# FFN down-projection of a one-core transformer layer computed as seven Strassen block products, with two plain column pairs at the head of each FFN

## The chip, the cores and the metric

The kernel runs on one core of one Trainium2 chip. The metric is the device time of one execution in microseconds (us); smaller is better. The engines are named as the profile names them: PE (TensorE, matrix products), PEld (its weight loads), DVE (VectorE), ACT (ScalarE), POOL (GpSimd), SP (SyncE, whose queue issues all bulk transfers of this kernel). Each runs its own instructions in a fixed order and waits for the others by semaphores.

## The reference, cut to what matters

One layer on 1024 tokens of width 1024, all in float32: a half-weighted SwiGLU FFN, a token mixer (two attention branches, unchanged here), and a second half-weighted FFN, each behind an RMS norm, and a final norm.

```python
D_MODEL, SEQ, D_FF = 1024, 1024, 2816

def swiglu(h, w1, w3, w2):
    return (jax.nn.silu(h @ w1) * (h @ w3)) @ w2
...
    x = x + 0.5 * swiglu(rmsnorm(x, ffn1_norm), ffn1_w1, ffn1_w3, ffn1_w2)
    x = x + token_mix(rmsnorm(x, mix_norm), ...)
    x = x + 0.5 * swiglu(rmsnorm(x, ffn2_norm), ffn2_w1, ffn2_w3, ffn2_w2)
    return rmsnorm(x, final_norm)
```

## The kernel before, in words

Activations lie transposed: features on the 128 partitions, tokens along the free axis, in two token halves `tb` of 512. The width 1024 is KD = 8 tiles of 128; the hidden width 2816 is NF = 22 tiles `f`, taken as 11 pairs. Every product is made with a number split in two: `split` writes a rounded `hi` (ACT, line 86) and the rest `lo` (DVE, line 82), and hi·hi + hi·lo + lo·hi makes three matmuls of 128x128 by 128x512 (`mm3`, lines 49 to 51).

An FFN has an up stage (`ffn_up`) and a down stage (`ffn_down`).

- Up stage. The first f pair is plain: 2 halves x 2 f x 2 matrices x 8 k x 3 = 192 matmuls. Its first half uses the input before it is scaled by the RMS factor R (R multiplies the result); then `scale_h` scales the second half and the first, and `right_sums` makes the input sums that Strassen's scheme (Winograd's form) needs (`T`, tiles `tf`). Pairs 1 to 10 follow as seven block products of 24 matmuls each, 168 per pair, into PSUM banks X, Y and Z; the weight sums of a pair are made by POOL (lines 327 to 330), on DVE in the first such pair. `finish_a` multiplies the gate (line 349, POOL). The results `a` go to DRAM (`s_a`).
- Down stage. For each half, for each of 22 f: load `a` (256 KB) and the rows of w2 (512 KB), split both, and add into 8 PSUM accumulators: 2 x 22 x 8 x 3 = 1056 matmuls. The last three f of a half are held back (`L_LAST`) and run one accumulator at a time, so that each can be added to x (line 412) and passed on (norm statistics, or the final output) while the next runs.

The order on every engine is set at build time by a scheduler, from the program's order, priorities and its own estimate of times; buffers come free as the last reader finishes (pools). Waits inside SP's queue hold back every transfer behind them.

Of the kernel before, what the change touches and what calls it, by code (L numbers as in the profile page):

```python
# [125 lines left out]
def norm_split(K, tb, k, gi):  # L126
    nc = K.nc
    x = K.x[tb][k]
    g = K.gain[:, gi, k:k + 1]
# [2 lines left out]
    nc.scalar.activation(out=hi, in_=x, func=AF.Copy, scale=g)
# [9 lines left out]
def norm_stat(K, tb, k, eng=None, hold=False):  # L142
    nc = K.nc
    x = K.x[tb][k]
    if k == 0:
        K.acc[tb] = K.np.tile([P, TB], F32, tag="nacc", name="nacc")
        nc.scalar.activation(out=K.acc[tb], in_=x, func=AF.Square)
    else:
        sq = K.np.tile([P, TB], F32, tag=f"nsq{tb * K.sq2}", name="nsq")
# [1 line left out]
        (eng or nc.gpsimd).tensor_tensor(out=K.acc[tb], in0=K.acc[tb], in1=sq, op=ALU.add)
# [4 lines left out]
def norm_final(K, tb):
    nc = K.nc
    with K.tc.high_priority(offset=HOT):
        tot = K.pt.tile([P, TB], F32, tag="acc", name="tot")
        nc.tensor.matmul(tot, lhsT=K.ones, rhs=K.acc[tb], start=True, stop=True)  # L160
# [4 lines left out]


def tail_stat(K, c, k):
    nc = K.nc
# [3 lines left out]
    if k == 0:
        K.tacc = sq
    elif k < KD - 1:
        nc.vector.tensor_tensor(out=K.tacc, in0=K.tacc, in1=sq, op=ALU.add)
# [74 lines left out]
def ffn_up(K, w13, tp, ctx0, gi, first):  # L250
# [12 lines left out]
    def store(f, tb, t):  # L263
        nc.sync.dma_start(out=K.s_a[tb][f], in_=t)

    with ExitStack() as c1:
        sb = open_pool(K, c1, "up_s", 3, side="right")
        ws = first if first else [load_fresh(K, n, w13[n // 2, n % 2]) for n in range(4)]
        K.nw = 4
        for tb in range(NTB):  # L270
            for f in range(2):
                u = [bank("XY"[f], m) for m in range(2)]
                for m in range(2):
                    for k in range(KD):
# [8 lines left out]
                nc.vector.tensor_tensor(out=t, in0=u[1], in1=t, op=ALU.mult)  # L283
# [4 lines left out]
    ctx0.close()
    with ctx:
        rw = open_pool(K, ctx, "up_raw", 1)  # L290
        po = open_pool(K, ctx, "up_post", 1)
        raw = lambda n: rw.tile([P, KD, P], F32, tag=n, name=n)
        B11, B21, B22 = K.h[0][0:h], K.h[0][h:], K.h[1][h:]

        def prod(o, w, m, x, start):
            for k in range(h):
                for i, (a, b) in enumerate(((0, 0), (0, 1), (1, 0))):
                    nc.tensor.matmul(o, lhsT=w[a][:, m * h + k], rhs=x[k][b], start=start and k == 0 and i == 0,  # L298
                                     stop=k == h - 1 and i == 2, skip_group_check=True)
# [55 lines left out]

def ffn_down(K, w2, xsrc, after, tail):
    nc = K.nc
    with ExitStack() as ctx:
# [8 lines left out]
        K.wpools = K.wpools + [open_pool(K, ctx, "whl3", B_W, side="right")]  # L367
        queue = []

        def fetch():  # L370
# [1 line left out]
            if n < NTB * NF:
                t = ar.tile([P, TB], F32, tag="ar", name="ar")
                nc.sync.dma_start(out=t, in_=K.s_a[n // NF][n % NF])
                a = [ah.tile([P, TB], F32R, tag=g, name=g) for g in ("ah", "al")]
                split(nc, a[0], a[1], t)
                queue.append((load_fresh(K, n, w2[n % NF]), a))
        fetch()
        fetch()
        for tb in range(NTB):  # L380
            acc = None
            held = []
            for f in range(NF):
                fetch()
                w, a = queue[tb * NF + f]
                if f >= 2 and f % 2 == 0 and f // 2 <= KD:
                    k = f // 2 - 1
                    nc.sync.dma_start(out=K.x[tb][k], in_=xsrc(tb, k))
                if acc is None:
                    acc = [pa.tile([P, TB], F32, tag="acc", name="acc") for _ in range(KD)]  # L390
                if f < NF - L_LAST:
                    late = tb == 1 and f < 2
                    for d in range(KD - late):
                        mm3(nc, acc[d], w, d, a, f == 0, False, True)
                    if late:
                        held.append((w, a))
                        if f == 1:
                            norm_final(K, 0)
                            if tail is not None:
                                tail(0, slice(0, TB))  # L400
                            for i, (w, a) in enumerate(held):
                                mm3(nc, acc[KD - 1], w, KD - 1, a, i == 0, False, True)
                            held = []
                else:
                    held.append((w, a))
            cols = [slice(0, TB)] if tail is None or tb == 0 else [slice(0, HB), slice(HB, TB)]
            for c in cols:
                for d in range(KD):
                    for i, (w, a) in enumerate(held):
                        mm3(nc, acc[d][:, c], w, d, [t[:, c] for t in a], False, i == L_LAST - 1, True)  # L410
                    x = K.x[tb][d][:, c]
                    nc.vector.scalar_tensor_tensor(out=x, in0=acc[d][:, c], scalar=0.5, in1=x, op0=ALU.mult, op1=ALU.add)
                    if tail is None or tb == 0:
                        after(tb, d)
                    else:
# [1016 lines left out]
```

## Time and profile before

| what | value |
|---|---|
| time, median of 3 runs (lowest to highest) | 3072.87 us (3072.54 to 3073.18) |
| the profiled execution, its own time | 3074.79 us |
| its span (first to last instruction in the profile) | 3072.7 us |
| mean granted clock of TensorE | 0.982 |
| PE / DVE / ACT / POOL busy, share of the span | 95% / 60% / 41% / 27% |
| FFN 1: first matmul, first down matmul, last down matmul's end | 6.52, 475.58, 721.44 us |
| FFN 2: first up matmul, first down matmul, last down matmul's end | 2357.76, 2811.34, 3058.58 us |

Between 721 and 2358 us lie the mixer and the projections, which the change does not touch. A matmul row's duration in this profile is its time in the pipeline; the next starts long before it ends, so what a matmul costs is read from starts, not from durations.

### The profile page before, as it was taken

To read this page: it belongs to the slowest core of one execution; us is meant where nothing else is said; L and a number is where in the kernel's file an instruction comes from. 1 tells how busy PE (TensorE), PEld (TensorE's weight loads), DVE (VectorE), ACT (ScalarE), POOL (GpSimd) and SP (SyncE) were. 2 spreads that over 40 slices of the span, in tenths; PEclk is the share of its full clock that TensorE was granted. 3 is DMA by queue.
4 is the path that set the end of the run, shared out by engine and by line. 5 is a ranking of instruction groups with operands and counts; after the bars stand their busy time and mean duration, and the time that the engine had idled before them with its cause. 6 is when DMAs were issued, how large, how long until landed. Compare 5 with 4: busy or idle time off the path is not lost.

```text
span 3072.7 us, 39792 instructions
## 1 busy us (share of the span) xinstructions
PE 2925.8 (95%) x14490; PEld 2442.3 (79%) x14490; DVE 1838.1 (60%) x3057; ACT 1267.6 (41%) x2231; POOL 842.3 (27%) x687
## 2 busy tenths in 40 slices
PE   6999999999999999889899999999999899999998
PEld 5788887887888778777788888888777688887887
DVE  7655554445678467667677777766434855555354
ACT  6222223332323245345566666666434322223342
POOL 5333330000035222322233333222332433331000
PEclk9999999999999999999999999999999999999999
DMA  2222226444546645444432234222832122225442
GB/s 103 93 83 83 82 69 235 159 144 140 158 158 224 214 142 181 162 168 155 140 111 83 83 123 149 83 76 89 303 124 91 56 83 83 82 83 199 154 167 66
DMA packets 168643, 397.95 MB, mean 130 GB/s; under 512 B 16000, under 2 KB 34688, under 8 KB 168448
## 3 DMA queue, kind: packets, MB, share of 16 engines
q1 hardware_dynamic: 168448, 395.42, 38.0%
q8 instruction: 114, 1.87, 0.3%
q14 instruction: 81, 0.66, 0.1%
HBM read 274.77 MB, written 120.59 MB: 129 GB/s over the span
## 4 chain that ended last, share of the span: by engine, by line
PE 78%; DVE 8%; DMA 6%; ACT 3%; issue 3%; POOL 2%; SPq 1%; DVEq 0%; ACTq 0%; POOLq 0%
PE Y L298 11%; PE X L298 7%; PE Z L298 7%; PE gm L49 6%; PE gm L51 6%; PE gm L50 6%; PE S L682 6%; PE acc L49 5%; PE acc L51 5%; PE acc L50 5%; PE tr L732 3%; PE o L886 2%; PE o L885 2%; DMA sg<-smx 1%; DMA wst<-in_win_dram 1%
## 5 line engine op out<-in xcount | busy, mean ns | idle before, releaser
L82 DVE TENSOR_TENSOR wlo<-wst,whi 128x1024 fp32r<-128x1024 f32 x183 | 238.1, 1303 | 233.6 <-ACT whi L86 223.3
L49 PE MATMUL gm<-hi,whi 128*128 128x512 f32 x880 | 352.5, 401 | 4.6 <-ACT whi L86 2.1
L51 PE MATMUL gm<-hi,wlo 128*128 128x512 f32 x880 | 348.9, 397 | 0.0
L50 PE MATMUL gm<-lo,whi 128*128 128x512 f32 x880 | 348.6, 396 | 0.0
L682 PE MATMUL S<-kt,qt 128*128 128x320 f32 (+5 forms) x1152 | 274.5, 352 | 44.2 <-ACT Pt L691 16.5
L298 PE MATMUL Y<-tf,whi 128*128 128x512 f32 x960 | 300.2, 394 | 1.0 <-ACT whi L86 1.0
L86 ACT ACTIVATE whi<-wst 128x1024 fp32r<-128x1024 f32 x147 | 155.1, 1058 | 333.0 <-PE acc L50 187.3
L86 ACT ACTIVATE th<-tr 128x512 fp32r<-128x512 f32 (+2 forms) x384 | 204.0, 543 | 200.9 <-PE tr L732 196.5
L82 DVE TENSOR_TENSOR tl<-tr,th 128x512 fp32r<-128x512 f32 (+2 forms) x384 | 236.6, 620 | 82.6 <-ACT th L86 78.9
L49 PE MATMUL acc<-ah,whi 128*128 128x512 f32 (+1 forms) x728 | 280.4, 385 | 4.5 <-DVE u L342 4.5
L51 PE MATMUL acc<-ah,wlo 128*128 128x512 f32 (+1 forms) x728 | 280.3, 385 | 0.0
L50 PE MATMUL acc<-al,whi 128*128 128x512 f32 (+1 forms) x728 | 279.7, 384 | 0.0
L689 DVE CUSTOM_DVE_ANT_0 S<-S,slab 128x896 f32<-128x896 f32 (+7 forms) x320 | 224.9, 709 | 69.3 <-PE S L682 64.0
L682 PEld LDWEIGHTS S<-kt,qt 128*128 128x128 f32 x1152 | 183.5, 190 | 67.8 <-ACT Pt L691 17.7
L839 POOL TENSOR_SCALAR Ps<-Ps,l 128x384 f32<-128x384 f32 (+7 forms) x128 | 100.7, 787 | 422.3 <-DVE l L837 209.9
L298 PEld LDWEIGHTS Y<-tf,whi 128*128 128x128 f32 x960 | 180.7, 188 | 43.0 <-ACT whi L86 1.4
L86 ACT ACTIVATE whi<-a 128x1024 fp32r<-128x1024 f32 x100 | 104.0, 1058 | 233.4 <-PE Y L298 157.7
L49 PEld LDWEIGHTS gm<-hi,whi 128*128 128x128 f32 x880 | 168.6, 192 | 37.5 <-ACT whi L86 2.3
L51 PEld LDWEIGHTS gm<-hi,wlo 128*128 128x128 f32 x880 | 168.2, 191 | 36.0 <-DVE wlo L82 0.3
L50 PEld LDWEIGHTS gm<-lo,whi 128*128 128x128 f32 x880 | 168.3, 191 | 31.5 <-issue 0.5
L82 DVE TENSOR_TENSOR wlo<-a,whi 128x1024 fp32r<-128x1024 f32 x100 | 173.9, 1753 | 26.3 <-ACT whi L86 26.3
L298 PE MATMUL Y<-tf,wlo 128*128 128x512 f32 x480 | 188.6, 394 | 0.0
(302 smaller groups left out, 6683.4 us busy)
## 6 DMA issues: line engine op xcount, KB each, us to landing
wst<-in_win_dram SPq DMA_DIRECT2D x55, 512.0 KB
wst<-in_f1w_dram SPq DMA_DIRECT2D x48, 512.0 KB
wst<-in_f2w_dram SPq DMA_DIRECT2D x48, 512.0 KB
ar<-sa SPq DMA_DIRECT2D x88, 256.0 KB
a<-in_f1w_dram SPq DMA_DIRECT2D x40, 512.0 KB
a<-in_f2w_dram SPq DMA_DIRECT2D x40, 512.0 KB
qt<-sq SPq DMA_DIRECT2D x128, 128.0 KB
qt<-sqn SPq DMA_DIRECT2D x64, 256.0 KB
```

What stands on the lines that cost most here:

```text
L49: first = nc.tensor.matmul(out, lhsT=w[0][:, wk], rhs=x[0], start=start, stop=False, skip_group_check=skip)
L50: nc.tensor.matmul(out, lhsT=w[0][:, wk], rhs=x[1], start=False, stop=False, skip_group_check=skip)
L51: nc.tensor.matmul(out, lhsT=w[1][:, wk], rhs=x[0], start=False, stop=stop, skip_group_check=skip)
L82: return nc.vector.tensor_tensor(out=lo, in0=src, in1=hi.bitcast(F32), op=ALU.subtract)
L86: nc.scalar.activation(out=hi, in_=src, func=AF.Copy)
L298: nc.tensor.matmul(o, lhsT=w[a][:, m * h + k], rhs=x[k][b], start=start and k == 0 and i == 0, stop=k == h - 1 and i == 2, skip_group_chec ...
L682: K.last = nc.tensor.matmul(S[:, o:o + n], lhsT=q, rhs=k[:, k0 + c:k0 + c + n], start=i == 0, stop=i == 1)
L689: nc.vector.tensor_tensor_reduce(out=sv, in0=sv, in1=mv, scale=-0.125, scalar=BIG, op0=ALU.add, op1=ALU.min, accum_out=nm)
L732: nc.tensor.transpose(tr[:, b * P:(b + 1) * P], src, K.ident)
L839: nc.gpsimd.tensor_scalar(out=p[:, 0:n], in0=p[:, 0:n], scalar1=l[:, c:c + 1], scalar2=1.0, op0=ALU.mult, op1=ALU.mult)
L885: nc.tensor.matmul(dst, lhsT=v, rhs=hi[:, b * P:(b + n) * P], start=False, stop=False, skip_group_check=True)
L886: nc.tensor.matmul(dst, lhsT=v, rhs=lo[:, b * P:(b + n) * P], start=False, stop=last, skip_group_check=True)
```

## The change

The down-projection becomes Strassen's seven products too, over the blocks (f of a pair) x (half of the output width) on the left and (f of the pair) x (token half) on the right. One product runs over all 11 pairs before the next begins ("streamed"), into four accumulators: 7 x 11 x 4 x 3 = 924 matmuls per FFN. The sums it needs are made during the up stage: `left_sums` loads both w2 tiles of a pair, makes S1 to S4 on DVE and writes them back to DRAM (`s_w`); `act_sums` makes T1 to T4 of the activations on POOL and writes them to `s_a`; for the plain pairs `plain_sums` reads the activations back first. The down stage loads per step two blocks of 256 KB into one buffer, so that one ACT and one DVE instruction of 1024 elements split both. Outputs are added to x from one or two of the products each (`outs`), 36 additions of 128x512 (or their halves) per FFN for 16. The norm statistics no longer need the order k = 0 to 7.

`NPLAIN = 2`: two f pairs are plain, 384 matmuls, in the order (half, pair) = (0,0), (0,1), (1,1), (1,0); Strassen pairs are 2 to 10.

```diff
+NPLAIN = 2
+def load_plain(K, pools, n, src):
+    st = K.wst.tile([P, KD, P], F32, tag="wst", name="wst")
+    K.nc.sync.dma_start(out=st, in_=src)
+    pool = pools[n % 2] if n < 4 else pools[2]
...
+    split(K.nc, hi, lo, st)
-        for tb in range(NTB):
+        ws = [first if first else [load_plain(K, plain, n, w13[n // 2, n % 2]) for n in range(4)]]
+        ws.append([load_plain(K, plain, n, w13[n // 2, n % 2]) for n in range(4, 8)])
+        for tb, p in ((0, 0), (0, 1), (1, 1), (1, 0)):
             for f in range(2):
-                u = [bank("XY"[f], m) for m in range(2)]
+                u = [bank("XYZ"[nu % 3], m) for m in range(2)]
...
-            if tb == 0:
-                scale_h(K, 0, gi, scale_h(K, 1, gi))
+            if (tb, p) == (0, 0):
+                gates = scale_h(K, 1, gi)
+            if (tb, p) == (0, 1):
+                scale_h(K, 0, gi, gates)
+        jobs = [lambda j=j: left_sums(K, ex, w2, j) for j in range(NF // 2)]
+        jobs[4:4] = [lambda p=p: plain_sums(K, ex, p) for p in range(NPLAIN)]
-        for fp in range(1, NF // 2):
+        for fp in range(NPLAIN, NF // 2):
...
+            for job in jobs[done[0]:done[1]]:
+                job()
...
-                finish_a(K, u[n, 0], u[n, 1], f, 1, store)
+                finish_a(K, u[n, 0], u[n, 1], f, 1, store if n == "u3" else lambda *_: None)
+            act_sums(K, u["c11", 0], u["u2", 0], u["c21", 0], u["u3", 0], u["c21", 1], u["u2", 1], u["u3", 1], fp)
+def act_sums(K, b11, b12, b21, b22, t1, t2, t4, j):
+    for out, a, b, n in ((t1, b12, b11, "T1"), (b12, b22, b12, "T3"), (t2, b22, t1, "T2"), (t4, b21, t2, "T4")):
+        nc.gpsimd.tensor_tensor(out=out, in0=a, in1=b, op=ALU.subtract)
+        nc.sync.dma_start(out=K.s_a[n][j], in_=out)
+def left_sums(K, ex, w2, j):
+    for i in range(2):
+        w.append(ex.tile([P, KD, P], F32, tag=f"w{i}", name="w2s"))
+        order_after(K, nc.sync.dma_start(out=w[i], in_=w2[2 * j + i]), K.mark)
+    a11, a21, a12, a22 = w[0][:, 0:h], w[0][:, h:], w[1][:, 0:h], w[1][:, h:]
+    for out, a, b, op in ((a22, a21, a22, ALU.add), (a21, a11, a21, ALU.subtract), (a11, a22, a11, ALU.subtract),
+                          (a12, a12, a11, ALU.subtract)):
+        nc.vector.tensor_tensor(out=out, in0=a, in1=b, op=op)
+    for i in range(2):
+        nc.sync.dma_start(out=K.s_w[j][i], in_=w[i])
+PRODUCTS = (("A11", "B11", ((0, 0),)), ("S2", "T2", ((1, 0),)), ("S3", "T3", ((0, 1), (1, 1))),
+            ("A12", "B21", ((0, 0),)), ("A22", "T4", ((0, 1),)), ("S1", "T1", ((1, 0), (1, 1))), ("S4", "B22", ((1, 0),)))
 def ffn_down(K, w2, xsrc, after, tail):
...
+            st = raws[n % 2].tile([P, KD, P], F32, tag="wst", name="st")
+            nc.sync.dma_start(out=st[:, 0:h], in_=src[0][:, src[1] * h:(src[1] + 1) * h])
+            nc.sync.dma_start(out=st[:, h:], in_=K.s_a[r][j].rearrange("p (k c) -> p k c", c=P))
+            hi, lo = [pools[n % 4].tile([P, KD, P], F32R, tag=t, name=t) for t in ("whi", "wlo")]
+            split(nc, hi, lo, st)
...
+        for pi, (l, r, outs) in enumerate(PRODUCTS):
+            if pi not in (1, 2):
+                acc = [pa.tile([P, TB], F32, tag="acc", name="acc") for _ in range(h)]
+            for j in range(nj):
+                fetch()
...
+                if j < nj - L_LAST:
+                    for d in range(h):
+                        mm3(nc, acc[d], w, d, a, j == 0 and pi not in (1, 2), False, True)
...
+                    for tb, i in outs:
+                        x = K.x[tb][i * h + d][:, c]
+                        nc.vector.scalar_tensor_tensor(out=x, in0=acc[d][:, c], scalar=0.5, in1=x, op0=ALU.mult, op1=ALU.add)
```

What the scheduler makes of it, at three places. In the rows, names end in a number that tells buffers apart.

PE where the first half of the plain part of FFN 1 ends, before: the next matmuls read `hi_531`, the scaled tile of the second token half.

```order
L49 MATMUL Y_475<-hi_349,whi_336 128x512
L50 MATMUL Y_475<-lo_350,whi_336 128x512
L51 MATMUL Y_475<-hi_349,wlo_337 128x512
L49 MATMUL X_618<-hi_531,whi_271 128x512
L49 MATMUL X_619<-hi_531,whi_271 128x512
L49 MATMUL Y_672<-hi_531,whi_314 128x512
```

The same place now: after pair 0 (bank Z) comes pair 1 of the same half, with the unscaled tiles `hi_342`, `lo_343` again and new weights.

```order
L49 MATMUL Z_565<-hi_415,whi_402 128x512
L50 MATMUL Z_565<-lo_416,whi_402 128x512
L51 MATMUL Z_565<-hi_415,wlo_403 128x512
L49 MATMUL X_660<-hi_342,whi_486 128x512
L50 MATMUL X_660<-lo_343,whi_486 128x512
L51 MATMUL X_660<-hi_342,wlo_487 128x512
```

What moved: 96 matmuls that need no R stand between the unscaled and the scaled half.

POOL in a Strassen pair of the up stage, before: three gate products of a pair (`u3`, `c21`, `u2`; line 349), then the weight sums of the pair after the next (lines 327 to 330).

```order
L349 TENSOR_TENSOR c21_1081<-c21_1081,c21_1082 128x512
L349 TENSOR_TENSOR u3_1079<-u3_1079,u3_1080 128x512
L349 TENSOR_TENSOR u2_1077<-u2_1077,u2_1078 128x512
L327 TENSOR_TENSOR s1_1567<-a21_1565,a22_1566 128x1024
L328 TENSOR_TENSOR a21_1565<-a11_1563,a21_1565 128x1024
```

POOL in a Strassen pair now (408 is the gate product, 378 the activation sums, 352 on the weight sums):

```order
L408 TENSOR_TENSOR u2_1677<-u2_1677,u2_1678 128x512
L378 TENSOR_TENSOR c21_1682<-u2_1677,c11_1683 128x512
L378 TENSOR_TENSOR u2_1677<-u3_1679,u2_1677 128x512
L378 TENSOR_TENSOR u2_1678<-u3_1679,c21_1682 128x512
L378 TENSOR_TENSOR u3_1680<-c21_1681,u2_1678 128x512
L352 TENSOR_TENSOR s1_2217<-a21_2215,a22_2216 128x1024
L353 TENSOR_TENSOR a21_2215<-a11_2213,a21_2215 128x1024
```

What moved: T1, T3, T2, T4 stand between the last gate product and the weight sums, written over the pair's own work tiles (`c21`, `u2`, `u3`), which the next pair writes again.

SP in a Strassen pair, before (307 loads the weights w13, 264 stores results):

```order
L307 DMA a12_2311<-in_f1w13_dram 128x1024
L264 DMA sa1_10_203<-u2_1824 128x512
L307 DMA a21_2312<-in_f1w13_dram 128x1024
L307 DMA a22_2313<-in_f1w13_dram 128x1024
L264 DMA sa0_12_183<-c11_2079 128x512
```

SP there now (332 loads w13, 279 stores results, 379 the activation sums):

```order
L332 DMA a12_2214<-in_f1w13_dram 128x1024
L332 DMA a21_2215<-in_f1w13_dram 128x1024
L379 DMA saT1_4_219<-c21_1682 128x512
L379 DMA saT3_4_241<-u2_1677 128x512
L379 DMA saT2_4_230<-u2_1678 128x512
L379 DMA saT4_4_252<-u3_1680 128x512
L332 DMA a22_2216<-in_f1w13_dram 128x1024
L279 DMA saB11_5_176<-c11_1959 128x512
```

What moved: the load of a22 for a later pair stands behind four stores that wait for POOL; before, it followed that of a21 at once.

More of the change, by code (lines that the diff above doesn't have):

```diff
@@ L144, in norm_stat @@
     x = K.x[tb][k]
-    if k == 0:
+    if tb not in K.seen:
+        K.seen[tb] = 0
         K.acc[tb] = K.np.tile([P, TB], F32, tag="nacc", name="nacc")
@@ L151, in norm_stat @@
         (eng or nc.gpsimd).tensor_tensor(out=K.acc[tb], in0=K.acc[tb], in1=sq, op=ALU.add)
-    if k == KD - 1 and not hold:
+    K.seen[tb] += 1
+    if K.seen[tb] == KD and not hold:
         norm_final(K, tb)
@@ L169, in tail_stat @@
     x = K.x[1][k][:, c]
-    sq = K.np.tile([P, HB], F32, tag="tsq0" if k == 0 else f"tsq{k % 3 + 1}", name="tsq")
+    acc = K.acc[1][:, c]
+    sq = K.np.tile([P, HB], F32, tag=f"tsq{k % 2}", name="tsq")
     nc.scalar.activation(out=sq, in_=x, func=AF.Square)
[L172 to L175, printed above, removed]
+    if k < KD // 2 - 1:
+        nc.vector.tensor_tensor(out=acc, in0=acc, in1=sq, op=ALU.add)
     else:
         tot = K.pt.tile([P, TB], F32, tag="acc", name="tot")[:, 0:HB]
-        nc.tensor.matmul(tot, lhsT=K.ones, rhs=K.tacc, start=True, stop=False)
+        nc.tensor.matmul(tot, lhsT=K.ones, rhs=acc, start=True, stop=False)
         nc.tensor.matmul(tot, lhsT=K.ones, rhs=sq, start=False, stop=True)
-        m = K.np.tile([P, HB], F32, tag="tsq1", name="nm")
+        m = K.np.tile([P, HB], F32, tag="tsq0", name="nm")
         nc.vector.tensor_scalar(out=m, in0=tot, scalar1=1.0 / D, scalar2=EPS, op0=ALU.mult, op1=ALU.add)
-        newton_rsqrt(nc, K.R[1][:, c], K.tacc, m, nc.vector)
+        newton_rsqrt(nc, K.R[1][:, c], acc, m, nc.vector)
 def split_fresh(K, n, src):
@@ L247, in right_sums, with ffn_up @@
     return T
-def ffn_up(K, w13, tp, ctx0, gi, first):
+def load_plain(K, pools, n, src):
+    st = K.wst.tile([P, KD, P], F32, tag="wst", name="wst")
+    K.nc.sync.dma_start(out=st, in_=src)
+    pool = pools[n % 2] if n < 4 else pools[2]
+    hi = pool.tile([P, KD, P], F32R, tag="whi", name="whi")
+    lo = pool.tile([P, KD, P], F32R, tag="wlo", name="wlo")
+    split(K.nc, hi, lo, st)
+    return hi, lo
+NPLAIN = 2
+def ffn_up(K, w13, w2, ctxt, ctx0, gi, first):
     nc = K.nc
@@ L297, in prod @@
                 for i, (a, b) in enumerate(((0, 0), (0, 1), (1, 0))):
-                    nc.tensor.matmul(o, lhsT=w[a][:, m * h + k], rhs=x[k][b], start=start and k == 0 and i == 0,
-                                     stop=k == h - 1 and i == 2, skip_group_check=True)
-        for fp in range(1, NF // 2):
+                    K.mark = nc.tensor.matmul(o, lhsT=w[a][:, m * h + k], rhs=x[k][b], start=start and k == 0 and i == 0,
+                                              stop=k == h - 1 and i == 2, skip_group_check=True)
+        for fp in range(NPLAIN, NF // 2):
             f0, f1 = 2 * fp, 2 * fp + 1
@@ L330, in ffn_up @@
             se.tensor_tensor(out=s4, in0=a12, in1=a11, op=ALU.subtract)
+            done = (fp - NPLAIN) * len(jobs) // (NF // 2 - NPLAIN), (fp + 1 - NPLAIN) * len(jobs) // (NF // 2 - NPLAIN)
+            for job in jobs[done[0]:done[1]]:
+                job()
             for src, x, n in ((a11, T[1], "u2"), (a21, T[2], "u3"), (a22, T[3], "c21")):
@@ L361, in ffn_down @@
         K.x = [[xp.tile([P, TB], F32, name=f"xd{tb}_{k}") for k in range(KD)] for tb in range(NTB)]
-        ar = open_pool(K, ctx, "ar", 4, side="right")
-        ah = open_pool(K, ctx, "ah", L_LAST + 3, side="right")
+        pools = K.wpools + [open_pool(K, ctx, f"whl{i}", B_W, side="right") for i in (3, 4)]
+        raws = [K.wst, open_pool(K, ctx, "wst2", 2, side="right")]
         pa = open_pool(K, ctx, "acc", 8, True)
@@ L371, in fetch @@
             n = len(queue)
[L372 to L381, printed above, removed]
+            if n == len(PRODUCTS) * nj:
+                return
@@ L382, in ffn_down @@
+            hi, lo = [pools[n % 4].tile([P, KD, P], F32R, tag=t, name=t) for t in ("whi", "wlo")]
+            split(nc, hi, lo, st)
+            queue.append(((hi, lo), [t[:, h:].rearrange("p k c -> p (k c)") for t in (hi, lo)]))
+        for _ in range(3):
+            fetch()
+        acc = None
+        for pi, (l, r, outs) in enumerate(PRODUCTS):
             held = []
-            for f in range(NF):
+            if pi not in (1, 2):
+                acc = [pa.tile([P, TB], F32, tag="acc", name="acc") for _ in range(h)]
+            for j in range(nj):
@@ L384, in ffn_down @@
                 fetch()
[L385 to L403, printed above, removed]
+                w, a = queue[pi * nj + j]
@@ L404, in ffn_down @@
+                if pi < 3 and j < h:
+                    for tb, i in outs:
+                        nc.sync.dma_start(out=K.x[tb][i * h + j], in_=xsrc(tb, i * h + j))
+                if j < nj - L_LAST:
+                    for d in range(h):
+                        mm3(nc, acc[d], w, d, a, j == 0 and pi not in (1, 2), False, True)
                 else:
                     held.append((w, a))
-            cols = [slice(0, TB)] if tail is None or tb == 0 else [slice(0, HB), slice(HB, TB)]
@@ L407, in ffn_down @@
-            for c in cols:
-                for d in range(KD):
+                if pi == 5 and j == 4:
+                    norm_final(K, 0)
+                    if tail is not None:
+                        tail(0, slice(0, TB))
+            last = pi == len(PRODUCTS) - 1
+            for c in [slice(0, HB), slice(HB, TB)] if last and tail is not None else [slice(0, TB)]:
+                for d in range(h):
                     for i, (w, a) in enumerate(held):
                         mm3(nc, acc[d][:, c], w, d, [t[:, c] for t in a], False, i == L_LAST - 1, True)
[L411 to L415, printed above, removed]
+                    for tb, i in outs:
+                        x = K.x[tb][i * h + d][:, c]
+                        nc.vector.scalar_tensor_tensor(out=x, in0=acc[d][:, c], scalar=0.5, in1=x, op0=ALU.mult, op1=ALU.add)
+                    if pi in (3, 4, 5):
+                        after(int(pi == 5), d + h * (pi != 3))
+                    elif last and tail is None:
+                        after(1, d)
+                    elif last:
@@ L416, in ffn_down @@
                         tail_stat(K, c, d)
-                    if d == KD - 1 and tail is not None and tb:
-                        tail(tb, c)
+                if last and tail is not None:
+                    tail(1, c)
 def ffn(K, w13, w2, ctx0, gi, first, xsrc, after, tail=None):
@@ L425, in ffn @@
         with ExitStack() as c1:
-            ffn_up(K, w13, open_pool(K, c1, "tf", 1, side="right"), ctx0, gi, first)
+            ffn_up(K, w13, w2, c1, ctx0, gi, first)
         ffn_down(K, w2, xsrc, after, tail)
@@ L1258, in body @@
     K.tc, K.nc, K.A = tc, nc, A
-    K.low, K.vv, K.gate, K.fill = 0, {}, None, None
+    K.low, K.vv, K.gate, K.fill, K.seen = 0, {}, None, None, {}
     K.h, K.acc, K.R = [None] * 2, [None] * 2, [None] * 2
```

46 lines of the change are left out of this document (33 added, 13 removed).

## Prediction

> **What bounds the kernel now.** I read the page's first part and the chain, then PE's starts in the timeline, then PE's waits stage by stage. PE is busy 95% of the span and carries 78% of the chain; the other engines have room.
>
> ```profile
> PE 2925.8 (95%) x14490; PEld 2442.3 (79%) x14490; DVE 1838.1 (60%) x3057; ACT 1267.6 (41%) x2231; POOL 842.3 (27%) x687
> PE 78%; DVE 8%; DMA 6%; ACT 3%; issue 3%; POOL 2%; SPq 1%; DVEq 0%; ACTq 0%; POOLq 0%
> L298 PE MATMUL Y<-tf,whi 128*128 128x512 f32 x960 | 300.2, 394 | 1.0 <-ACT whi L86 1.0
> ```
>
> The 394 ns of that group is a matmul's time in the pipeline, not its price. The price comes from the chain in order of time: the same run of 24 X matmuls stands once per Strassen pair, so two of its starts, seven pairs apart, give the period.
>
> ```profile
> 168.23 5.52 PE X L298 x24
> ...
> 439.57 5.52 PE X L298 x24
> ...
> 2503.99 5.52 PE X L298 x24
> ```
>
> (439.57 - 168.23) / 7 = 38.76 us for 168 matmuls: **230.7 ns each**.
>
> Stage limits, from PE's timeline (start, duration, idle before):
>
> ```profile
> 6.52 1.22 PE L49 MATMUL X<-hi,whi 128*128 128x512 f32 x2 [6.52 <-ACT hi L132]
> ...
> 475.58 0.39 PE L49 MATMUL acc<-ah,whi 128*128 128x512 f32 x1
> ...
> 478.82 0.50 PE L49 MATMUL acc<-ah,whi 128*128 128x512 f32 x1 [2.27 <-DVE u L342]
> ...
> 726.37 1.22 PE L160 MATMUL tot<-nacc,ones 128*128 128x512 f32 x1 [4.93 <-DVE nacc L151]
> ...
> 2357.76 0.47 PE L49 MATMUL X<-hi,whi 128*128 128x512 f32 x1
> ```
>
> Down stage of FFN 1: from 475.58 to 726.37 - 4.93 = 721.44 is 245.9 us; less the wait of 2.27, 1056 matmuls take 243.6: 230.7 ns again. So both large stages run at PE's pace. What PE loses lies at the head of each FFN (waits by releaser: us, times, longest), the first four of FFN 1, the rest of FFN 2:
>
> ```profile
> PE X L298 <- DVE wlo L82: 7.4, 1, 7.4
> PE X L49 <- ACT hi L86: 7.3, 1, 7.3
> PE X L49 <- ACT hi L132: 6.5, 1, 6.5
> PE Y L49 <- DVE s L283: 6.0, 1, 6.0
> ...
> PE Z L298 <- ACT whi L86: 4.5, 1, 4.5
> PE X L50 <- DVE lo L82: 4.3, 2, 4.1
> PE X L298 <- DVE s L283: 4.0, 1, 4.0
> ```
>
> After such a wait PE also runs slow for some us; in the stage table (PE, PEld, DVE, ACT, POOL busy, PEclk, DMA share, GB/s) the granted clock falls to half:
>
> ```profile
> 40.00:50.00 10.00, 3.64 (x7) 2.12 (x8) 10.00 (x10) 9.67 (x19) 8.38 (x6) 0.50 0.07 26
> 80.00:90.00 10.00, 9.85 (x31) 7.83 (x32) 9.25 (x14) 2.98 (x6) 1.24 (x1) 0.71 0.42 140
> ```
>
> The loss as a whole: to the X run of the third Strassen pair stand 192 + 2 x 168 + 12 = 540 matmuls, 124.6 us, and four `tot` products (about 0.45 each; two in FFN 2). FFN 1 takes 168.23 - 6.52 = 161.7, **35.3 more**; FFN 2 takes 2503.99 - 2357.76 = 146.2, **20.7 more**.
>
> **The change, part by part.**
>
> *Down stage, matmuls.* 1056 - 924 = 132 fewer per FFN, 264 x 0.2307 = **-60.9 us**, if PE stays the limit. The Trainium skill (TensorE: Matmul & The Clock Gate, Back-to-back issue gap) gives two other prices for 512 columns, about 216 ns isolated and about 131 ns in a sustained stream; by these the 264 would be worth 57 or 35 us. The trace shows neither (230.7 in both stages), and decides. A step is now 12 matmuls, 2.77 us, and in it DVE splits 1024 elements, ACT too:
>
> ```profile
> L82 DVE TENSOR_TENSOR wlo<-wst,whi 128x1024 fp32r<-128x1024 f32 x42 | 52.0, 1239 | 108.3 <-ACT whi L86 108.3
> L412 DVE SCALAR_TENSOR_TENSOR xd<-acc,xd 128x512 f32<-128x512 f32 x16 | 11.0, 688 | 8.6 <-PE acc L51 8.6
> L86 ACT ACTIVATE whi<-wst 128x1024 fp32r<-128x1024 f32 x43 | 45.4, 1059 | 117.0 <-PE acc L50 102.2 <-DMA wst<-in_f1w_dram 14.7
> ```
>
> DVE: 11 x 1.239 + at most 8 x 0.688 = 19.1 us per product of 30.5. ACT: 11.6. POOL idle. Transfers: 2 x 256 KB per 2.77 us is 189 GB/s; the trace has shown 347 at this very place:
>
> ```profile
> 476.00:500.00 24.00, 21.73 (x94) 17.46 (x95) 12.80 (x16) 11.16 (x13) 1.29 (x1) 1.00 0.98 347
> ```
>
> The 16 loads of x (256 KB each, in SP's queue among steps 11 to 19) add 4 MB, 12 us at that rate; eight split buffers and four raw ones let the loads run ahead. I cost both at 0; with a cover gone the bound is 12 us per FFN.
>
> *Product boundaries.* Products 2 and 3 go on in the accumulators that DVE has just read, so PE could wait for the fourth addition, up to one split and one addition, 1.9 us, at two places per FFN. Other work of the next step stands before it on PE. Between 0 and 7.7; I take **+2**. The wait of 2.27 at the second accumulator goes: the first accumulator that waits for DVE is now the fourth, 2.1 us later in PE's order. Between 0 and -4.5; I take **-4.5**.
>
> *Second plain pair.* 192 - 168 = 24 matmuls more per FFN: 48 x 0.2307 = **+11.1**. It puts 96 matmuls, 22.1 us, ahead of the first that needs scaled input. Will that cover the scaling? R of the second half, DVE's scaling and splitting, and the end of PE's first 96 in FFN 1, and the first scaling in FFN 2:
>
> ```profile
> 35.55 0.69 DVE L122 TENSOR_TENSOR R<-R,nacc 128x512 f32<-128x512 f32 x1
> ...
> 38.26 8.81 DVE L209 SCALAR_TENSOR_TENSOR x<-x,gain,R 128x512 f32<-128x512 f32 x8
> ...
> 47.59 10.94 DVE L82 TENSOR_TENSOR lo<-x,hi 128x512 fp32r<-128x512 f32 x10
> ...
> 32.45 0.39 PE L51 MATMUL Y<-hi,wlo 128*128 128x512 f32 x1
> ...
> 2372.64 2.45 DVE L209 SCALAR_TENSOR_TENSOR xx<-xx,gain,R 128x512 f32<-128x512 f32 x2
> ```
>
> Four more weight splits on DVE (4 x 1.24, some in its gaps) put R at about 39. Begun at 41, the eight scalings end at 50 and the eight `lo` at 60, one per 1.1 us. PE ends its first 96 at 32.8 as before and 192 at 55; the `lo` are needed from 55 to 60, one per 0.7 us. It is covered by a hair. In FFN 2 the same splits, 5.0, and a plain result that now stands ahead of R put the scaling at about 2381, its end 20 us later at 2401; PE needs it from 2357.8 + 192 matmuls and two `tot` = 2403. So nearly all of 35.3 + 20.7 = 56.0 should go. What stays: FFN 1's start-up at half clock while x arrives (32.8 against 30.5 worked out, 2.3), and the first Strassen pair's weight sums, made on DVE in a row of six at 1.23 behind the last plain result, against 11.1 us of X products: spare 3 or none. I take **-50** of the 56 (bounds 0 and -53.7).
>
> *Sums in the up stage.* Per Strassen pair POOL gets four products of 128x512, DVE four or eight, SP six to ten transfers. The stage table of one pair, POOL's and DVE's nearest rows, and ACT's split of a weight sum:
>
> ```profile
> 323.35:362.01 38.66, 38.66 (x169) 31.53 (x169) 19.85 (x18) 10.79 (x14) 15.28 (x7) 1.00 0.26 80
> ...
> 308.65 2.40 POOL L329 TENSOR_TENSOR a<-s,a 128x1024 f32<-128x1024 f32 x1 [4.73 <-DVE wlo L82]
> 316.68 2.28 POOL L349 TENSOR_TENSOR u<-u,u 128x512 f32<-128x512 f32 x1
> 324.21 1.28 POOL L349 TENSOR_TENSOR u<-u,u 128x512 f32<-128x512 f32 x1 [5.25 <-issue]
> 337.20 2.40 POOL L327 TENSOR_TENSOR s<-a,a 128x1024 f32<-128x1024 f32 x1 [11.71 <-DVE wlo L82]
> ...
> 324.31 2.26 DVE L82 TENSOR_TENSOR wlo<-a,whi 128x1024 fp32r<-128x1024 f32 x1 [0.23 <-ACT whi L86]
> 327.02 1.23 DVE L82 TENSOR_TENSOR wlo<-a,whi 128x1024 fp32r<-128x1024 f32 x1 [0.45 <-ACT whi L86]
> ...
> 325.93 1.06 ACT L86 ACTIVATE whi<-a 128x1024 fp32r<-128x1024 f32 x1 [1.65 <-PE X L298]
> ```
>
> POOL works 15.3 us of the pair's 38.7. Its last gate product ends at 325.5; then it idles until 337.2, when DVE frees a buffer. Four sums at 1.28 to 2.28 end by 331 to 335: they fit in that hole, and the weight sums behind them start no later. SP holds a22's load behind their stores; with a landing of 3 to 6 us it is there by 334 to 341 where 337 is wanted. Those 4 us are spare: a sum made at 311.1 is split at 325.9, when PE frees a buffer; PE's new order wants it 12 matmuls earlier, which leaves 12. T3 overwrites a tile that DVE fills again once 48 matmuls of the next pair are done, 11.1 us after 323.4, at 334.5; it is made by 328 to 330, stored by 336 at the latest, and PE waits only if that slips 5 us more. DVE's four sums (0.69 each) find it half idle. So **0**; bounds 0 and one lost split (2.26 - 1.23 = 1.03) in each of 18 pairs, 18.5.
>
> *Ends.* The wait of 4.93 before `tot` and the tail after the last product hold the same chain of operations: 0.
>
> Sum: -60.9 + 2 - 4.5 + 11.1 - 50 = **-102.3**. The profiled execution took 3074.79 (span 3072.7, 2.1 around it), 1.9 over the median of 3072.87; so 2972.5 in its terms, **2971** against the median.
>
> **The rivals.**
> 1. *The head's waits only move.* What waits now is scaling plus Strassen sums on DVE, which is 100% busy from 40 to 50; the second pair adds splits to that engine. The margins above are under 2 us, which speaks for it; that the work needs no more than the 22.1 us of cover speaks against. Half of the 56 kept: about 2996; all: 3021.
> 2. *Pairs stretch*, because DVE and POOL hold each other up (2.26 for 1.23, 2.28 for 1.28 where they meet), now with four more instructions each. Against it stands POOL's hole of 11.7 us. One lost split per pair gives 2971 + 18.5 = 2990. The Trainium skill (SBUF — State Buffer, 🔬 SBUF: two separate sides) states the rule behind it: a GpSimd operation and a VectorE operation with two SBUF inputs exclude each other for the whole instruction. By that rule, which these rows bear out, 15.3 + 5.1 of POOL and 11.4 of DVE (seven splits, four sums) never overlap, 31.8 of 38.8 us: tight, but not the limit.
> 3. *Slower:* the down stage falls to the latency of its loads. A raw buffer is held from issue until split; with four, steps lengthen once load, ACT and DVE exceed 4 x 2.77 = 11.1 us, and the whole gain of 102 is gone at 2.77 + 102 / 154 = 3.43 us per step, a cycle of 13.7. The longest landings on the chain:
>
> ```profile
> 1383.38 13.89 DMA kt<-sk
> ...
> 2.58 6.04 DMA wst<-in_f1w_dram
> ```
>
> The first, with 1.06 and 1.24 added, would make a cycle of 16.2, steps of 4.05 and a time of 2971 + 154 x 1.28 = 3168; but it is a scattered 512 KB. The second is a plain load in a full queue and makes 8.3.
>
> **How the numbers follow.** Near 2971 (2960 to 2984): 0.67. Rival 1: 0.16, rival 2: 0.12. Rival 3: 0.04 slower than before, 0.01 about even. The low end adds the bounds of gains not taken (3.7 at the head, 2 at boundaries, and a few us of the 4.93): 2960. The high end takes in half of rivals 1 and 2: 2999. A difference under 0.2%, 6 us, is what this measurement cannot tell from none: faster 0.95, same 0.01, slower 0.04.
>
> **What would show it.** The X runs of the Strassen pairs still 38.8 us apart; the third pair's near 140 instead of 168 and near 2490 instead of 2504; no wait of PE over 3 us between the halves of the head; the down stage 213 to 217 us without DMA waits; `tot` still waiting about 5. Wrong: PE waits on `u` or `whi` in every pair, or on st's loads in the down stage.

## The result and the profile after

| | before | changed |
|---|---|---|
| time, median (lowest to highest) | 3073.02 us (3072.54 to 3078.1) | 2999.14 us (2994.09 to 3007.84) |
| profiled execution (span) | 3074.79 us (3072.7) | 3003.5 us (3001.7) |

The ratio is 0.976 (0.973 to 0.979): 74 us faster, where 102 were forecast. The page's first part:

```profile
PE 2872.7 (96%) x14238; PEld 2395.9 (80%) x14238; DVE 1956.4 (65%) x3140; ACT 1274.2 (42%) x2195; POOL 979.9 (33%) x765
```

PE has 252 instructions fewer, DVE and POOL 118 and 138 us more. PE's timeline gives the borders of the stages (start, duration, engine, line; in brackets the idle time before and what ended it). In the order of the rows: first matmul of FFN 1, first Strassen matmul, first of the down stage, last of the down stage; then the same four of FFN 2.

```profile
6.83 0.80 PE L49 MATMUL Y<-hi,whi 128*128 128x512 f32 x1 [6.83 <-ACT hi L132]
...
101.18 0.39 PE L323 MATMUL X<-hi,whi 128*128 128x512 f32 x1
...
465.28 0.39 PE L49 MATMUL acc<-whi 128*128 128x512 f32 x1
...
680.73 0.40 PE L51 MATMUL acc<-whi,wlo 128*128 128x512 f32 x1
...
2319.34 0.47 PE L49 MATMUL Y<-hi,whi 128*128 128x512 f32 x1
...
2409.27 0.39 PE L323 MATMUL X<-hi,whi 128*128 128x512 f32 x1
...
2772.13 0.39 PE L49 MATMUL acc<-whi 128*128 128x512 f32 x1
...
2986.87 0.28 PE L51 MATMUL acc<-whi,wlo 128*128 128x256 f32 x1
```

Against the borders of before (in the table of the time and profile before), profiled execution against profiled execution:

| stage | before | changed | difference | forecast |
|---|---|---|---|---|
| up stages, FFN 1 + 2 | 469.06 + 453.58 | 458.45 + 452.79 | -11.4 | -38.9 |
| down stages | 245.86 + 247.24 | 215.85 + 215.02 | -62.2 | -63.4 |
| between the FFNs | 1636.32 | 1638.21 | +1.9 | 0 |
| start, tail, around the span | | | +0.4 | 0 |
| sum | | | -71.3 | -102.3 |

The down stages are worth what was forecast. Of the missing 31 us, 27.5 are in the up stages, and there not in the plain part: its 384 matmuls and the `tot` products are worth 90.4 us in FFN 1 and 89.5 in FFN 2 at 230.7 ns, and took 94.35 and 89.93. The nine Strassen pairs are worth 1512 x 0.2307 = 348.8 us. They took 364.10 (101.18 to 465.28) and 362.86 (2409.27 to 2772.13): **29.3 us lost**, where before they ran at 38.8 a pair. PE's waits in FFN 1 from 100 to 470 us (us, times, longest; the row of `acc` belongs to the start of the down stage, the others to the pairs):

```profile
PE Y L323 <- DVE u L363: 4.6, 4, 1.9
PE Z L323 <- DVE u L370: 2.8, 2, 1.4
PE Y L323 <- DVE wlo L82: 1.9, 1, 1.9
PE acc L49 <- DVE u L370: 1.8, 1, 1.8
PE Z L323 <- DVE wlo L82: 0.2, 1, 0.2
```

Lines 363 and 370 are DVE's additions that read a product out of a PSUM bank and so free it. Before, no pair waited for them. One such wait and what stands ahead of it, first on POOL, then on DVE, then on PE (a duration on DVE or POOL includes the time in which the instruction is held):

```profile
404.26 2.79 POOL L352 TENSOR_TENSOR s<-a,a 128x1024 f32<-128x1024 f32 x1 [9.01 <-DVE wlo L82]
407.13 3.24 POOL L353 TENSOR_TENSOR a<-a,a 128x1024 f32<-128x1024 f32 x1
...
404.10 0.69 DVE L400 TENSOR_TENSOR w2s<-w2s 128x512 f32<-128x512 f32 x1
404.70 0.68 DVE L363 TENSOR_TENSOR u<-Y,s 128x512 f32<-128x512 f32 x1
405.31 2.83 DVE L82 TENSOR_TENSOR wlo<-s,whi 128x1024 fp32r<-128x1024 f32 x1
408.06 2.86 DVE L400 TENSOR_TENSOR w2s<-w2s 128x512 f32<-128x512 f32 x1
410.85 0.68 DVE L363 TENSOR_TENSOR u<-Y,s 128x512 f32<-128x512 f32 x1
...
411.58 0.74 PE L323 MATMUL Y<-tf,whi 128*128 128x512 f32 x2 [1.94 <-DVE u L363]
```

POOL has room, as forecast (idle for 9.01 us). Then it makes two weight sums in a row. DVE's split started in the first and ended 1.1 us after it; then a sum of `left_sums` (line 400), 0.69 us by itself, got in behind POOL's second and ended 0.55 us after that (410.37): 2.86 us. The addition behind it in DVE's order had its operands, and PE waited for it. The wait cost more than its own 1.94 us: PE's next matmuls ran slower (the last section shows the clock, and that this does not follow every such wait), and the pair (stretch between two X runs, columns as in the stage table of the prediction) took 43.0 us at a granted clock of 0.96:

```profile
383.75:426.76 43.01, 41.07 (x170) 32.50 (x169) 26.68 (x25) 11.29 (x14) 25.78 (x12) 0.96 0.48 165
```

All nine waits on line 363 in the two FFNs have the same rows ahead of them: a split of 2.8 us, then an S sum of 2.86 to 2.88 us. Ahead of each of the four waits on line 370 (1.42 us each) stand an S sum that took 1.80 to 2.06 us beside a weight sum, and two more S sums of 0.69.

The S sums also delay PE in a second, smaller way, without POOL. An S sum waits for its own load from DRAM, and a split that stands behind it on DVE waits with it; its `whi` was ready at 2586.6 (DVE, then PE):

```profile
2589.21 0.69 DVE L400 TENSOR_TENSOR w2s<-w2s 128x512 f32<-128x512 f32 x1 [5.07 <-DMA w2s<-in_f2w_dram]
2589.82 1.22 DVE L82 TENSOR_TENSOR wlo<-s,whi 128x1024 fp32r<-128x1024 f32 x1
...
2591.09 0.50 PE L323 MATMUL Z<-tf,wlo 128*128 128x512 f32 x1 [1.75 <-DVE wlo L82]
```

There are three such waits in the changed kernel's pairs (0.21, 1.75 and 0.68), 2.6 us in all.

### The profile page after: what moved, and what is told of

It reads as the page before. It is cut to its first block, busy times and chain, and to the rows that moved or that the text cites. A ratio compares the mean times of both kernels' runs of the same rounds, so it can differ in the third digit from the quotient of the medians.

```text
span 3001.7 us, 39937 instructions
## 1 busy us (share of the span) xinstructions
PE 2872.7 (96%) x14238; PEld 2395.9 (80%) x14238; DVE 1956.4 (65%) x3140; ACT 1274.2 (42%) x2195; POOL 979.9 (33%) x765
## 3 DMA queue, kind: packets, MB, share of 16 engines
q8 instruction: 112, 1.84, 0.3%
## 5 line engine op out<-in xcount | busy, mean ns | idle before, releaser
L323 PE MATMUL Y<-tf,whi 128*128 128x512 f32 x864 | 275.0, 397 | 9.8 <-DVE u L363 9.8
L82 DVE TENSOR_TENSOR wlo<-st,whi 128x1024 fp32r<-128x1024 f32 x154 | 198.2, 1304 | 119.6 <-ACT whi L86 119.0
L49 PE MATMUL acc<-whi 128*128 128x512 f32 (+1 forms) x628 | 243.4, 388 | 3.3 <-DVE u L370 3.3
L50 PE MATMUL acc<-wlo,whi 128*128 128x512 f32 (+1 forms) x628 | 243.4, 388 | 0.0
L51 PE MATMUL acc<-whi,wlo 128*128 128x512 f32 (+1 forms) x628 | 243.1, 389 | 0.0
L86 ACT ACTIVATE whi<-st 128x1024 fp32r<-128x1024 f32 x154 | 160.5, 1057 | 186.9 <-PE acc L51 124.6
L82 DVE TENSOR_TENSOR wlo<-a,whi 128x1024 fp32r<-128x1024 f32 x90 | 159.8, 1779 | 83.1 <-ACT whi L86 79.8
L323 PEld LDWEIGHTS Y<-tf,whi 128*128 128x128 f32 x864 | 162.6, 189 | 51.4 <-DVE u L363 14.7
L323 PE MATMUL Y<-tf,wlo 128*128 128x512 f32 x432 | 171.0, 397 | 2.8 <-DVE wlo L82 2.8
L950 PE MATMUL o<-th,vt 128*128 128x256 f32 (+1 forms) x608 | 164.5, 287 | 1.8 <-ACT th L86 1.7
```

The source lines that it names most:

```text
L49: first = nc.tensor.matmul(out, lhsT=w[0][:, wk], rhs=x[0], start=start, stop=False, skip_group_check=skip)
L50: nc.tensor.matmul(out, lhsT=w[0][:, wk], rhs=x[1], start=False, stop=False, skip_group_check=skip)
L51: nc.tensor.matmul(out, lhsT=w[1][:, wk], rhs=x[0], start=False, stop=stop, skip_group_check=skip)
L82: return nc.vector.tensor_tensor(out=lo, in0=src, in1=hi.bitcast(F32), op=ALU.subtract)
L86: nc.scalar.activation(out=hi, in_=src, func=AF.Copy)
L323: K.mark = nc.tensor.matmul(o, lhsT=w[a][:, m * h + k], rhs=x[k][b], start=start and k == 0 and i == 0, stop=k == h - 1 and i == 2, skip_g ...
```

## The experiments

Theory A: the S sums on DVE are the cause, by the way just shown. Its rival inside (A1) is that DVE simply has more to do. Theory B: the T sums on POOL. Theory C: the new transfers, in SP's queue or as traffic. "Loss" is the time of the nine pairs beyond 348.8 us, in FFN 1 and FFN 2 of the profiled execution.

| run | time | ratio to before (interval) | loss |
|---|---|---|---|
| changed | 2999.1 | 0.9759 (0.9730-0.9788) | 15.3 + 14.0 |
| e9: changed again | 2994.6 | 0.9760 (0.9744-0.9775) | 10.9 + 15.0 |
| e1: no S sums | 2970.0 | 0.9663 (0.9649-0.9678) | 2.1 + 1.0 |
| e2: no T sums | 2990.0 | 0.9727 (0.9712-0.9741) | 9.8 + 12.0 |
| e3: neither | 2966.6 | 0.9650 (0.9634-0.9666) | 0 + 0 |
| e4: S on POOL | 2980.9 | 0.9701 (0.9687-0.9716) | 1.9 + 1.3 |
| e5: weight sums halved | 2977.6 | 0.9693 (0.9679-0.9707) | 1.7 + 3.1 |
| e6: weight sums on DVE | 2975.4 | 0.9687 (0.9671-0.9704) | 1.2 + 2.5 |
| e7: e4, banks Z, X, Y | 2975.6 | 0.9689 (0.9674-0.9703) | 1.0 + 1.0 |
| e8: e4, one plain pair | 3017.2 | 0.9824 (0.9807-0.9841) | |
| e10: e6, banks Z, X, Y | 2976.6 | 0.9699 (0.9684-0.9714) | 4.2 + 2.7 |
| e11: e5, banks Z, X, Y | 2976.0 | 0.9695 (0.9680-0.9710) | 1.9 + 2.8 |

**e1, e2, e3: which sums.**

```diff
 def left_sums(K, ex, w2, j):                     # e1, e3
-        nc.vector.tensor_tensor(out=out, in0=a, in1=b, op=op)
+        pass
 def act_sums(...):                               # e2, e3
-        nc.gpsimd.tensor_tensor(out=out, in0=a, in1=b, op=ALU.subtract)
-        nc.sync.dma_start(out=K.s_a[n][j], in_=out)
+        nc.sync.dma_start(out=K.s_a[n][j], in_=b)
```

> Leaves out DVE's four subtractions and additions of left_sums (S1 to S4); their loads and stores stay, so the down stage multiplies unsummed weights. Theory A (a sum on DVE stands ahead of an addition that frees a PSUM bank, and is itself held up to 2.9 us by a POOL weight sum of 2.8 to 3.2 us): the ten or so waits of PE on line 363 and 370 go, pairs fall from 40.4 to 38.8-39.2 us, the time by 20 to 29 us to 2970-2980. Theory B (the four new sums on POOL are the load that is too much): pairs stay above 40, time within 6 us of the changed kernel. Theory C (the new transfers): no change either.

> Leaves out POOL's four subtractions of act_sums (T1 to T4); their stores stay and write one operand. Theory A: the waits on lines 363 and 370 stay, since the weight sums of POOL and the S sums on DVE still meet; at most 8 us of the 29 go: 2990-2999. Theory B: pairs fall to 38.8-39.2 us, time to 2970-2980.

> Leaves out both groups of sums; all loads and stores stay. A and B: pairs at 38.7-38.9 us, 2968-2975. Theory C (transfers make the pairs long): pairs stay at 39.5 or more, 2985 or more.

Without the S sums 26 of the 29 us are gone and the time is 2970, the forecast's 2971; PE's only waits in e1's pairs are 2.0 and 0.8 us in the first pair of each FFN. The T sums alone are worth 4 to 8 us of loss (against e9 and the changed kernel): with them gone, the S sums still meet POOL's weight sums, and 20 of the 88 took 2.28 to 2.89 us. e2's 2990.0 is the lower edge of theory A's range. All transfers stay in e3, and no wait of PE is left in its pairs (38.75 us each; the time is 1.4 us below the range given): C falls, and B as the main cause.

**e4: the S sums on POOL**, nothing left out.

```diff
-        nc.vector.tensor_tensor(out=out, in0=a, in1=b, op=op)
+        nc.gpsimd.tensor_tensor(out=out, in0=a, in1=b, op=op)
```

> Makes S1 to S4 on POOL instead of DVE, nothing left out. Theory A: POOL has a hole of 8.6 to 9 us per pair and does not hold itself up; DVE's additions are free of them: pairs 39 to 39.5, time 2975-2987. If what counts is the sum of POOL's work and DVE's SBUF work, wherever it stands: no gain, 2993-3010.

The stretch of the nine pairs, first in the changed kernel, then in e4:

```profile
101.18:465.28 364.10, 354.45 (x1513) 285.18 (x1512) 223.81 (x209) 96.47 (x117) 200.58 (x98) 0.99 0.49 171
```

```profile
101.08:451.82 350.74, 348.99 (x1513) 283.70 (x1512) 181.57 (x166) 96.66 (x116) 256.20 (x141) 1.00 0.50 174
```

POOL is now busy (or held) 256 of 351 us, more than before, and yet the pairs are short. A sum held on POOL delays weight sums, which have slack (PE's only waits in e4's pairs are 1.7 and 0.8 us, for splits in the first pair); held on DVE it delays PSUM.

**e5, e6: hold or load?** Against A1, theory A2 says that what counts is how long an instruction of POOL can hold one of DVE. The changed kernel with the S sums on DVE, and POOL's weight sums cut in halves (e5), or made on DVE too (e6).

```diff
+            for c in (slice(0, h), slice(h, KD)) if fp > NPLAIN else (slice(0, KD),):      # e5
-            se.tensor_tensor(out=s1, in0=a21, in1=a22, op=ALU.add)
+                se.tensor_tensor(out=s1[:, c], in0=a21[:, c], in1=a22[:, c], op=ALU.add)
 ... (and so the other three)
-            se = nc.vector if fp == NPLAIN else nc.gpsimd                                  # e6
+            se = nc.vector
```

> The changed kernel with S1 to S4 on DVE as they are, but POOL's four weight sums of a pair cut into eight of half the length. Theory A2 (a DVE sum with two operands in SBUF is held for the rest of a POOL instruction, so what counts is how long that instruction is): holds of at most 1.5 us instead of 2.9, PE's waits on lines 363 and 370 fall from 17 to about 6 us, the time by 8 to 20 us to 2980-2991. Theory A1 (what counts is DVE's added 2.8 us per pair and its place in the order): no gain, 2994-3005.

> The changed kernel with S1 to S4 on DVE as they are, and the weight sums of all Strassen pairs on DVE too (4 x 1.23 = 4.9 us more per pair there, none of POOL's instructions of 2.4 to 3.2 us left). Theory A2: pairs shorten to 39 to 39.8 us, 2975-2990. Theory A1: DVE's load grows from 24 to 29 us of 40, pairs lengthen, 3005-3030.

Both did better than A1 allows: e6 came out at the good end of A2's range, e5 2.4 us below it. In e6 DVE has 4.9 us more work in every pair but the first than in the changed kernel (busy, holds included, in FFN 1's nine pairs: 233.75 us for 223.81), and the ratio is 0.7% lower. In e5 the order of the instructions in the pairs is that of the changed kernel on PE and on DVE, so no new order explains its gain. The group of the S sums on DVE (busy, mean ns of one), changed, e5, e6:

```profile
L400 DVE TENSOR_TENSOR w2s<-w2s 128x512 f32<-128x512 f32 x88 | 91.3, 1037 | 50.8 <-DMA w2s<-in_f2w_dram 26.4 <-DMA w2s<-in_f1w_dram 24.1
```

```profile
L401 DVE TENSOR_TENSOR w2s<-w2s 128x512 f32<-128x512 f32 x88 | 84.4, 960 | 48.7 <-DMA w2s<-in_f2w_dram 25.4 <-DMA w2s<-in_f1w_dram 23.0
```

```profile
L400 DVE TENSOR_TENSOR w2s<-w2s 128x512 f32<-128x512 f32 x88 | 64.6, 734 | 36.5 <-DMA w2s<-in_f2w_dram 19.1 <-DMA w2s<-in_f1w_dram 17.3
```

The mean falls little in e5: more sums are lengthened (31 of the 88 took over 0.75 us, 16 in the changed kernel), but none took more than 1.84 us, where 12 took about 2.87. The same place as above, in e5:

```profile
394.89 3.92 POOL L353 TENSOR_TENSOR s<-a,a 128x512 f32<-128x512 f32 x2 [8.93 <-DVE wlo L82]
398.77 3.44 POOL L354 TENSOR_TENSOR a<-a,a 128x512 f32<-128x512 f32 x2
...
395.34 0.68 DVE L364 TENSOR_TENSOR u<-Y,s 128x512 f32<-128x512 f32 x1
395.94 1.72 DVE L82 TENSOR_TENSOR wlo<-s,whi 128x1024 fp32r<-128x1024 f32 x1
397.58 1.78 DVE L401 TENSOR_TENSOR w2s<-w2s 128x512 f32<-128x512 f32 x1
399.29 0.68 DVE L364 TENSOR_TENSOR u<-Y,s 128x512 f32<-128x512 f32 x1
```

The sum is through after 1.78 us instead of 2.86, because DVE gets its turn between two halves; the addition starts 4.0 us after the one before it (395.34), not 6.15, and PE no longer waits for such an addition in the pairs. So the length of the other engine's instruction decided, not DVE's load. What is left in e5 and e6 is in part the second way: splits behind an S sum that waits for its load cost PE 2.4 and 1.1 us.

**e7, e10, e11: the seam to the down stage.** e4 waits 3.0 and 3.1 us at the fourth accumulator, where the changed kernel waits 1.82 and 1.51. From ACT, DVE and PE in e4:

```profile
454.05 1.06 ACT L86 ACTIVATE whi<-st 128x1024 fp32r<-128x1024 f32 x1 [6.14 <-DMA st<-saB]
...
455.14 1.23 DVE L82 TENSOR_TENSOR wlo<-st,whi 128x1024 fp32r<-128x1024 f32 x1 [3.79 <-ACT whi L86]
456.28 0.68 DVE L370 TENSOR_TENSOR u<-Z,u 128x512 f32<-128x512 f32 x1
...
457.02 0.50 PE L49 MATMUL acc<-whi 128*128 128x512 f32 x1 [3.00 <-DVE u L370]
```

The last Z product ended at 452; its addition stands behind the split of the third down step, whose load landed at 454. e7 lays the up stage's PSUM banks out so that the first four accumulators are not on a Z bank; e10 and e11 do the same to e6 and e5.

```diff
     K.nw = 0
+    for n in "ZXY":
+        bank(n, 0), bank(n, 1)
```

> As the kernel with S1 to S4 on POOL (2981), and the six PSUM banks of the up stage are laid out in the order Z, X, Y, so that the first four accumulators of the down stage do not fall on a Z bank. If the fourth accumulator's wait of 3.0 us per FFN is for that bank alone: 2974-2977. If the late third load (its split stands ahead of the addition on DVE) then holds PE instead: 2979-2982.

> All weight sums on DVE (2975) and the PSUM banks of the up stage in the order Z, X, Y. The two waits of the fourth accumulator (1.55 and 0.82) go, unless the late load takes their place: 2972-2975.

> POOL's weight sums in halves (2978) and the banks in the order Z, X, Y: one wait of 0.94 less, 2975-2978.

The wait for the bank is gone in e7, and about half of it comes back as waits for the late load's split itself:

```profile
455.40 0.50 PE L49 MATMUL acc<-whi 128*128 128x512 f32 x1 [0.84 <-ACT whi L86]
456.66 0.50 PE L50 MATMUL acc<-wlo,whi 128*128 128x512 f32 x1 [0.76 <-DVE wlo L82]
```

e7's 2975.6 lies in the range for the bank alone, but its gain over e4, from 0.9701 to 0.9689, is inside the intervals; so are the differences of e10 to e6 and of e11 to e5. e10 missed its range by 1.6 us. Which of e5, e6, e7, e10 and e11 is best is open; all beat the changed kernel, at 2975 to 2978.

**e8: the second plain pair.**

```diff
-NPLAIN = 2
+NPLAIN = 1
-        for tb, p in ((0, 0), (0, 1), (1, 1), (1, 0)):
+        for tb, p in ((0, 0), (1, 0)):
...
+            if (tb, p) == (0, 0):
+                scale_h(K, 0, gi, scale_h(K, 1, gi))
```

> As the kernel with S1 to S4 on POOL (2981), with one plain pair and ten Strassen pairs, order (half 0, half 1) as before the change. If the second plain pair covers the scaling as predicted (50 us of waits for 11 of matmuls): 3015-3025. If the waits only moved: 2970-2990.

0.9824 against e4's 0.9701: the second plain pair is worth 38 us, against 39 in the forecast (50 less 11.1). With one pair PE waits at the head again, the longest 7.4 and 6.7 us (before 7.4 and 7.3). The further waits are not all the same as before, but in all FFN 1 loses 26.8 us in them up to the third pair (before 24.3). From 30 to 110 us:

```profile
PE X L320 <- DVE wlo L82: 7.4, 1, 7.4
PE X L49 <- ACT hi L86: 6.7, 1, 6.7
PE X L50 <- DVE lo L82: 6.6, 1, 6.6
PE Z L320 <- DVE wlo L82: 4.3, 1, 4.3
```

**e9: the changed kernel again**, on the chip of e10 and e11.

> The changed kernel again, on the chip of the two below, so that they stand beside it: 2994-3005, ratio 0.973 to 0.979.

The ratio is the same. The loss in FFN 1 is 10.9 us instead of 15.3, though as many S sums take over 1.6 us there (eight) and PE's waits are only 1.0 us shorter. The other 3.5 us are slower matmuls: PE was busy for 350.99 us in those pairs, and for 354.45 in the changed kernel's execution. The granted clock shows why (last section).

## Why the prediction was right, and where it was off

- **Down matmuls, -60.9: right.** 215.85 and 215.02 us per stage, in the range of 213 to 217; 924 x 0.2307 = 213.2, and the only wait in it is the one at the fourth accumulator. No wait of PE for a load appears, so rival 3 is out.
- **Product boundaries +2, and -4.5 for the accumulator's wait: the sum held, the second was half wrong.** At the boundaries 1.2 us is left over after the waits (215.85 + 215.02 - 426.3 - 3.3). The wait did not go: it moved to the fourth accumulator (1.82 and 1.51, before 2.27 each). The step took the bank to be free 2.1 us later than needed, and did not see that DVE's addition would be queued behind a split that waits for a load; e4 and e7 show that.
- **Head, -50 of 56, and +11.1: right.** The plain parts lose 4.0 and 0.4 us; with the first pair's waits for its weight splits (1.94, 0.84) 7.2 are left where 6.0 were kept. Rival 1 is out, by e8 too.
- **Sums in the up stage, 0 with an upper bound of 18.5: the step that failed.** Measured 29.3 - 2.8 = 26.5 us, more than its bound. The rows of the hold were on the table (2.26 for 1.23). The step then priced it by busy time, POOL's hole of 11.7 us and "DVE half idle", and bounded it by one lost *split* per pair, 1.03. But the instruction that was added on DVE is short, and can be held for all of a POOL weight sum of 2.4 to 3.2; and what is queued behind it on DVE is an addition that frees PSUM. It is rival 2's mechanism, at 1.4 times its price: 2990 there, 2999 measured, at the end of the stated range. "PE waits on `u`", named as what would show the forecast wrong, is what came, though in 10 of the 18 pairs and not in every one. The hold on the S sums is the main part of it, the wait for their loads (2.6 us) another that the step did not price.
- **The range: held in part by luck.** Its high end, 2999, took in half of rivals 1 and 2. Rival 1, whose half is worth 25 us, did not come at all; rival 2 had a chance of 0.12 and came larger than its price. As a sum the two halves would give 2971 + 25 + 9 = 3005, not 2999.
- **The rule on the shared ports.** DVE's sum of 0.69 us took 2.86 where POOL's instruction held it. That is the exclusive hold for the whole instruction which the Trainium skill states (SBUF — State Buffer, 🔬 SBUF: two separate sides). The forecast used the rule as a sum over a pair (31.8 of 38.8 us, "tight, but not the limit"), and by that sum e4, where the four S sums take at least 1.28 us each on POOL for 0.69 on DVE, should have done no better. The rule bites by single instructions and by what stands behind them.
- **The signs.** The X runs of the pairs are 38.2 to 43.0 us apart instead of 38.8. The third pair's stands at 143.41 (forecast 140) and 2448.85. The 2490 given for the latter left out what FFN 1 gains before it, over 50 us by the prediction's own terms.
- **Ends, 0.** `tot` waits 4.44 (before 4.93), the tail is 0.4 longer. Between the FFNs, where nothing was changed, 1.9 us are left over in this execution; their cause was not looked for.

With the S sums out of DVE's way (e1, 2970.0) the whole of the other terms comes out at the forecast's 2971: one term was mis-sized.

## What to carry to other kernels

Before a short instruction is added to an engine that is "half idle", look at what it can be held by (here the longest instruction with SBUF operands on the other engine, not the mean), at what it waits for itself (here its load) and at what is queued behind it: if that is the instruction which frees a PSUM bank, a hold can go on to PE. Three cures did about equally well: put the new work on the engine that holds, cut that engine's long instructions in two, or bring all such sums onto one engine even though it gets busier. And a wait that "goes" because a buffer is needed later has to be followed in the order of the engine that frees it.
